# The second layer's MLP: in each quarter the first pair of down chunks takes eight of its 16 k tiles in seven products

## The chip, the cores and the metric

The kernel runs on one NeuronCore of a Trainium2 chip. The metric is the device time of one execution in microseconds (us), as the median of several runs. A profiled execution of the kernel before was also recorded; its own time is given below beside the medians.

The engines are named as in the profile: PE is TensorE (matmuls; PEld are its weight loads), DVE is VectorE, ACT is ScalarE, POOL is GpSimd, SP is SyncE, which issues most of the transfers from HBM.

## The reference

The reference is a decoder trunk of two layers on 256 tokens of width 2048, all in float32. Each layer has a token mixer (layer 0 a gated MLP with spatial mixing, layer 1 a state-space layer), a cross-attention to a memory of 256 tokens, and an MLP, each behind an RMS norm and with a residual add; a final RMS norm ends it. The change lies in the MLP of layer 1:

```python
def squared_relu_mlp(h, w_up, w_down):
    return jnp.square(jax.nn.relu(h @ w_up)) @ w_down
...
    x = x + squared_relu_mlp(rms_norm(x, g_ff[i]), f_w_up[i], f_w_down[i])
```

`h` is 256 x 2048, `w_up` 2048 x 8192, `w_down` 8192 x 2048.

## The kernel before, in words

**Float32 out of three matmuls.** Every float32 operand is split into a high part, which is the value cast to float32r, and a low part, which is the rest. A product is then high x high + low x high + high x low, three matmuls where one would do. `split` (L103, L104) makes the two parts: ScalarE casts the high part (`whi`, `own`, `hh`), VectorE subtracts it from the source for the low part (`wlo`, `own`, `hl`). Weights come from HBM in tiles of 128 x 1024 float32 (512 KB): two k tiles of 128 rows by 512 columns. They arrive in raw buffers `wraw` (four) and are split into `whi` and `wlo` (three buffers each).

**The MLP** (`mlp`, L630 on) goes through the 8192 hidden features in four quarters `b` of 2048. A quarter first computes its up products: four chunks `n` of 512 features, two calls of `gemm_feat` (L163 to L191) each, whose result is evicted by a copy on ScalarE and an add on VectorE, squared behind the relu (L649) and split into `hh` and `hl`, the tokens' operand of the down product. Then come the quarter's down products: the 2048 hidden features are 16 k tiles, the 2048 output columns are four chunks of 512, and each chunk's result is added to the residual `x` by `gather` (L666).

**Seven products.** In layer 1 the down chunks are taken in pairs by `gemm_seven` (L705 on), except for the last two chunks of the last quarter. For a pair the operands of the first four k tiles form a 2 x 2 by 2 x 2 block product: two token halves `t` of 128, two halves `i` of the k tiles (two k tiles each), two output chunks `j`. It would take eight block products; by the scheme of Strassen in Winograd's form it takes seven, four of them with sums of token blocks. A block product is six matmuls of 128 x 128 by 128 x 512 (two k tiles, three matmuls each). The k tiles behind the first four are taken straight (`direct`, `whole`): one weight tile serves both token halves, twelve matmuls.

The sums on the tokens' side are made once per quarter by `token_sums` (L691 on) from the first up chunk, and split: `sums`. The sums of weight blocks are made by VectorE as they are needed, in `run` and in one of the raw tiles `ws` (four buffers): run = B01 - B00, then run = B11 - run, B01 = B11 - B01, run = B10 - run. A weight block that meets `sums` is split into tiles `own`, of which there are two (L656):

```python
own = lambda: mp.tile([P, KB * NB], F32R, name="own", bufs=2)
```

`parts` takes one for the high and one for the low part, so that one such pair exists at a time. The other blocks go through `whi` and `wlo`. The products are, in the written order: 1 (`summed` 0, into the PSUM bank of token half 0 and chunk 1), 2 (`block`, bank (1, 0)), 3 (`block`, bank (0, 0)), 4 and 5 (`summed` 1 and 2, bank (1, 0)), 6 (`block`, bank (1, 0)), 7 (`summed` 3, bank (0, 1)). Between products 3 and 7 stand four direct tiles. What a bank holds after products 1, 2, 4 and 5 is also needed by itself: `keep` (L763) has ScalarE copy it to a tile `kept` of 128 x 512 before the next product adds to the bank. The copy after product 5 is `u3`:

```python
u3 = keep((1, 0), 3)
whole(0, 0)
v.tensor_tensor(out=run, in0=raw[1, 0], in1=run, op=ALU.subtract)
block((1, 0), 1, 1, run)
```

`whole(0, 0)` first writes bank (0, 0) with six matmuls, then bank (1, 0) with six.

**What sets the order.** The kernel is written as a flow of operations on tiles. A scheduler at build time orders the instructions of each engine by priority and by its own costs, hands out the buffers of the pools, and puts in the semaphore waits. Each engine then works through its list in that order, and a transfer waits in SP's list until its buffer is free. So the order on an engine can differ from the written one, and a change in one place can move its neighbours.

Of the kernel before, what the change touches and what calls it, by code (L numbers as in the profile page):

```python
# [16 lines left out]
P = 128  # L17
# [21 lines left out]
class Trunk:  # L39
# [454 lines left out]
    def attention(self, x, layer, cur, nxt):  # L494
# [3 lines left out]
        with tc.tile_pool(name="at", bufs=2, reuse_waits="tile") as ap:  # L498
# [67 lines left out]
            def values(h0):  # L566
# [16 lines left out]
                self.gemm_seven(tiles, token(memT), self.mem_sums, wv, h0, 0,  # L583
# [40 lines left out]
            for j in range(0, NCH, 2):  # L624
                self.gemm_seven(tiles, token(oT), sums[0], wo, j, 0, gather)
                for n in (j, j + 1):
                    self.at(1 + n - j, lambda n=n: nxt.chunk(x, n))


    def mlp(self, x, layer, cur, nxt):  # L630
# [3 lines left out]
        with tc.tile_pool(name="ml", bufs=4, reuse_waits="tile") as mp:  # L634
# [3 lines left out]
            kept = lambda i: mp.tile([P, NB], F32, name="kept", bufs=4)  # L638
            self.fifth = None if nxt.closing else mp
            for b in range(DFF // D):  # L640
                hid = []
                for n in range(NCH):
# [10 lines left out]
                    if nxt.closing and n == 0:  # L653
                        sums = self.token_sums(ws(), lambda: mp.tile([P, 4, 2, P], F32R, name="sums", bufs=2), *rs)
# [14 lines left out]
                for n in range(NCH):  # L669
                    end = b == DFF // D - 1  # L670
                    if nxt.closing and not (end and n >= NCH - 2):
                        if n % 2 == 0:
                            self.gemm_seven((ws, run, kept), lambda kt, t: [f[:, kt % 4, t * P:(t + 1) * P]
                                                                            for f in hid[kt // 4]],
                                            sums, wd, n, b * KT, gather, own=own)
                            if end:
                                nxt.start()
# [27 lines left out]
    def gemm_seven(self, tiles, token, sums, w, n0, k0, gather, end=None, own=None):  # L705
# [23 lines left out]
        def into(key, kts, left, hi, lo, end=False):  # L729
# [10 lines left out]
        def block(key, t, i, src, end=False):  # L740
            into(key, range(KB), lambda kk: token(KB * i + kk, t), *parts(src), end)

        def summed(key, k, src, end=False):
            into(key, range(KB), lambda kk: [f[:, k, kk, :] for f in sums], *parts(src, own), end)

        todo = {j: list(range(2, KT // KB)) for j in range(2)}
# [23 lines left out]
        run = run()  # L770
        v.tensor_tensor(out=run, in0=raw[0, 1], in1=raw[0, 0], op=ALU.subtract)
        summed((0, 1), 0, run, True)
        block((1, 0), 0, 0, raw[0, 0], True)
        m5, m1 = keep((0, 1), 0), keep((1, 0), 1)
        block((0, 0), 0, 1, raw[1, 0])
        whole(1, 1)
        v.tensor_tensor(out=run, in0=raw[1, 1], in1=run, op=ALU.subtract)
        summed((1, 0), 1, run, True)
# [4 lines left out]
        summed((1, 0), 2, raw[0, 1], True)  # L783
# [4 lines left out]
        block((1, 0), 1, 1, run)  # L788
        whole(1, 1)
        summed((0, 1), 3, raw[1, 1])  # L790
# [752 lines left out]
```

## Time and profile before

| | us |
|---|---|
| median of 3 runs | 2791.5 (2790.08 to 2792.14) |
| profiled execution, its own time | 2789.63 |
| span of its trace, first to last instruction | 2787.9 |

Busy time in the profiled execution: PE 99% of the span, DVE 71%, ACT 50%, POOL 8%; the granted PE clock is 0.999 of full speed, and the transfers run at 213 GB/s in the mean. The MLP of layer 1 takes the last quarter of the span: the four quarters' first pairs begin at 2170.34, 2344.19, 2518.05 and 2691.92 us from the span's start.

How to read the rows: a group of instructions has its line, engine, operation, output tile <- input tiles and shape, then the busy time and the mean in ns of one, then the idle time of its engine before it and who ended that. In a timeline a row has the start, the duration, engine, line and operation; in square brackets stands the idle time before and its releaser. The windows give the busy time of each engine in a stretch, with the number of its instructions. Matmuls overlap in time, so that their busy times do not add up to the time they take.

### The profile page before, as it was taken

Reading aid. Unit: us, or ns where it says so; the run is one execution under the profiler, and the core shown is the slowest. Engines: PE = TensorE matmul, PEld = TensorE weight load, DVE = VectorE, ACT = ScalarE, POOL = GpSimd, SP = SyncE. Lnnn points to the kernel's source line nnn. Section 1 sums busy time; section 2 is a strip of 40 time slices with the busy share of each in tenths; the row PEclk is TensorE's granted clock in tenths of the full one; section 3 lists DMA queues with packets and bytes.
Section 4 is the critical chain, followed back from the end, with each engine's and each line's share of the span. In section 5 each row is a group of like instructions: output and inputs, shape, how many; then the busy total and the mean of one; then the engine's idle time right before and its main releaser. Section 6 shows DMA issues by size and latency. Waiting matters only on the chain. (4 is left out here: it accounts for less than half of the span.)

```text
span 2787.9 us, 39690 instructions
## 1 busy us (share of the span) xinstructions
PE 2767.1 (99%) x15020; PEld 2331.6 (84%) x15020; DVE 1984.8 (71%) x2740; ACT 1396.2 (50%) x1805; POOL 234.4 (8%) x435
## 2 busy tenths in 40 slices
PE   9999999999999999999999999999999999999998
PEld 7888888888888888888887888888888888888887
DVE  6865756778978778787567657557776767667665
ACT  6545544554534434444556445445554545445454
POOL 0100000001022222221213100000000000000000
PEclk9999999999999999999999999999999999999999
DMA  8766655557788888887879767564556566565655
GB/s 294 232 209 217 200 179 181 175 158 244 211 260 260 255 259 262 257 259 226 240 242 270 217 199 239 176 191 159 179 158 216 170 212 204 164 221 167 213 187 158
DMA packets 196223, 593.76 MB, mean 213 GB/s; under 512 B 45120, under 2 KB 47216, under 8 KB 195520
## 3 DMA queue, kind: packets, MB, share of 16 engines
q1 hardware_dynamic: 151728, 531.17, 60.7%
q0 software_dynamic: 43776, 59.01, 7.8%
q8 instruction: 117, 1.92, 0.3%
q10 hardware_dynamic: 528, 1.06, 0.1%
q14 instruction: 74, 0.61, 0.1%
HBM read 567.51 MB, written 23.46 MB: 212 GB/s over the span
## 5 line engine op out<-in xcount | busy, mean ns | idle before, releaser
L104 DVE TENSOR_TENSOR wlo<-wraw,whi 128x1024 fp32r<-128x1024 f32 (+1 forms) x893 | 1085.9, 1221 | 490.4 <-ACT whi L103 484.8
L103 ACT CAST whi<-wraw 128x1024 fp32r<-128x1024 f32 (+1 forms) x893 | 937.3, 1052 | 857.0 <-PE acc L731 204.5
L174 PE MATMUL acc<-act,whi 128*128 128x512 f32 x3072 | 742.4, 392 | 0.6 <-ACT whi L103 0.6
L174 PEld LDWEIGHTS acc<-act,whi 128*128 128x128 f32 x3072 | 562.7, 188 | 111.5 <-issue 2.6
L179 PEld LDWEIGHTS acc<-act,wlo 128*128 128x128 f32 x3072 | 394.9, 191 | 18.6 <-DVE wlo L104 2.9
L179 PE MATMUL acc<-act,wlo 128*128 128x256 f32 x3072 | 403.9, 283 | 1.9 <-DVE wlo L104 1.5
L159 PE MATMUL acc<-whi,act 128*128 128x512 f32 x1472 | 369.8, 393 | 6.2 <-ACT whi L103 5.4
L159 PEld LDWEIGHTS acc<-whi,act 128*128 128x128 f32 x1472 | 275.1, 189 | 64.0 <-ACT whi L103 5.4
L731 PE MATMUL acc<-whi,act 128*128 128x512 f32 x864 | 233.0, 392 | 0.0
L815 PE MATMUL acc<-whi,hl 128*128 128x512 f32 x544 | 213.3, 392 | 0.0
L814 PE MATMUL acc<-whi,hh 128*128 128x512 f32 x544 | 212.7, 391 | 0.0
L159 PE MATMUL acc<-wlo,act 128*128 128x512 f32 x736 | 197.9, 391 | 0.0
L731 PEld LDWEIGHTS acc<-whi,act 128*128 128x128 f32 x864 | 160.3, 188 | 36.5 <-ACT ends L763 1.9
L159 PEld LDWEIGHTS acc<-wlo,act 128*128 128x128 f32 x736 | 138.6, 188 | 28.9
L731 PE MATMUL acc<-whi,hh 128*128 128x512 f32 x378 | 148.4, 393 | 0.0
L731 PE MATMUL acc<-whi,hl 128*128 128x512 f32 x378 | 147.1, 389 | 0.0
L817 PE MATMUL acc<-wlo,hh 128*128 128x512 f32 x544 | 145.9, 390 | 0.0
L731 PE MATMUL acc<-wlo,act 128*128 128x512 f32 x432 | 133.1, 390 | 0.0
L815 PEld LDWEIGHTS acc<-whi,hl 128*128 128x128 f32 x544 | 102.1, 188 | 23.1 <-issue 2.2
L190 ACT COPY r<-acc 128x512 f32<-128x512 f32 x64 | 37.6, 587 | 166.7 <-PE acc L174 166.7
L817 PEld LDWEIGHTS acc<-wlo,hh 128*128 128x128 f32 x544 | 102.1, 188 | 21.5 <-issue 0.2
L814 PEld LDWEIGHTS acc<-whi,hh 128*128 128x128 f32 x544 | 102.1, 188 | 21.4 <-issue 0.4
(369 smaller groups left out, 2762.4 us busy)
## 6 DMA issues: line engine op xcount, KB each, us to landing
wraw<-in_f_w_up SPq DMA_DIRECT2D x256, 512.0 KB, 4.6
wraw<-in_f_w_down SPq DMA_DIRECT2D x228, 512.0 KB, 4.6
wraw<-in_x_w_q SPq DMA_DIRECT2D x64, 512.0 KB, 4.1
wraw<-in_x_w_k SPq DMA_DIRECT2D x64, 512.0 KB, 4.4
wraw<-in_b_w_out SPq DMA_DIRECT2D x64, 512.0 KB, 4.4
wraw<-in_a_w_in SPq DMA_DIRECT2D x63, 512.0 KB, 4.1
wraw<-in_x_w_v SPq DMA_DIRECT2D x48, 512.0 KB, 4.2
wraw<-in_x_w_o SPq DMA_DIRECT2D x48, 512.0 KB, 4.3
```

What stands on the lines that cost most here:

```text
L103: self.nc.scalar.copy(out=hi, in_=src)
L104: return self.nc.vector.tensor_tensor(out=lo, in0=src, in1=hi.bitcast(F32), op=ALU.subtract).ins
L159: nc.tensor.matmul(out[t], a[:, kt, sl], b[:, kk, :], start=st and a is ah, stop=en)
L174: nc.tensor.matmul(acc[:, f, :], hi[:, kk, sl], both[:, kt].rearrange("p a s -> p (a s)"), start=first and kk == 0, stop=last and kk == FK ...
L179: nc.tensor.matmul(acc[:, f, 0:S], lo[:, kk, sl], ah[:, kt, :], start=False, stop=last and kk == FK - 1, skip_group_check=True)
L190: nc.scalar.copy(out=dst, in_=acc[:, :, S:])
L731: mm = lambda s, m, e: nc.tensor.matmul(out, s, m, start=key not in begun, stop=e, skip_group_check=True)
L814: nc.tensor.matmul(acc[:, t, :], ah, hi[:, kk, :], start=kt == 0, stop=False)
L815: nc.tensor.matmul(acc[:, t, :], al, hi[:, kk, :], start=False, stop=False)
L817: nc.tensor.matmul(acc[:, t, :], hid[kt // 4][0][:, kt % 4, sl], lo[:, kk, :], start=False, stop=kt == KT - 1)
```

## The change

In each quarter, the first pair of down chunks (`n` = 0) now takes eight of its 16 k tiles in seven products: the four k tiles behind the first four are a second block. Each of the seven products has two halves, one of either block, which add into the same bank. The second block's four raw weight tiles are loaded ahead by `block_ahead` into one large tile `more` (from the pool of the activations, whose buffer the attention has left), and three of its four weight sums are made there during the up products; the fourth is made in place in the GEMM. A second set of token sums comes from the second up chunk (`sums` has four buffers instead of two). The direct tiles of a first pair fall from twelve to eight. The `kept` tiles now lie in `more` too. The quarter's second pair is taken as before, with one block. In the attention the calls hand over the same sums as a list, which changes nothing there; those lines are left out below.

The scheduler places the rest. Three places in the first quarter's first pair, by engine, with output tile <- input tiles.

TensorE, from the fifth product (the third `summed`) to the work after it; the moving weights stand first, then the stationary tokens. Before:

```order
L731 MATMUL acc<-own,sums 128x512 x6
L731 MATMUL acc<-whi,hh 128x512
L731 MATMUL acc<-whi,hl 128x512
L731 MATMUL acc<-whi,hh 128x512
L731 MATMUL acc<-whi,hl 128x512
L731 MATMUL acc<-wlo,hh 128x512 x2
```

Now:

```order
L750 MATMUL acc<-own,sums 128x512 x6
L750 MATMUL acc<-wlo,hh 128x512 x2
L750 MATMUL acc<-own,sums 128x512 x6
L750 MATMUL acc<-whi,hh 128x512
L750 MATMUL acc<-whi,hl 128x512
```

The product's second half follows two matmuls behind its first, and the six matmuls with `hh` and `hl` that stood behind the product have moved ahead of it.

VectorE at the same place, with buffer numbers, since rows would read alike. Before:

```order
L104 TENSOR_TENSOR own_19905<-ws_19811,own_19904 128x1024
L666 SCALAR_TENSOR_TENSOR x_5605<-kept_19883,r2_18966,x_5605 128x512
L104 TENSOR_TENSOR wlo_19937<-run_19817,whi_19936 128x1024
L104 TENSOR_TENSOR wlo_19949<-wraw_19946,whi_19948 128x1024
L104 TENSOR_TENSOR own_19965<-ws_19815,own_19964 128x1024
```

Now:

```order
L104 TENSOR_TENSOR own_19959<-ws_19828,own_19958 128x1024
L673 SCALAR_TENSOR_TENSOR x_5605<-more_19605,r2_18966,x_5605 128x512
L795 TENSOR_TENSOR run_20146<-ws_20140,ws_20138 128x1024
L104 TENSOR_TENSOR wlo_20011<-more_19605,whi_20010 128x1024
L104 TENSOR_TENSOR own_19969<-more_19605,own_19968 128x1024
L104 TENSOR_TENSOR own_20039<-ws_19832,own_20038 128x1024
```

own_19905 was the low part of the fifth product's weights; own_19959 and own_19969 are those of its two halves, and between them now stand the next pair's first subtraction (L795) and the split of a tile for product 6 (wlo_20011).

ScalarE at the head of the GEMM; L190 is the copy that evicts the up's last product. Before:

```order
L103 CAST whi_19829<-ws_19809 128x1024
L103 CAST whi_19843<-ws_19813 128x1024
L190 COPY r_19693<-acc_19694 128x512
L103 CAST whi_19855<-wraw_19853 128x1024
L103 CAST own_19872<-run_19817 128x1024
L103 CAST hh_19596<-r_19693 128x512
```

Now:

```order
L103 CAST whi_19866<-more_19605 128x1024
L190 COPY r_19707<-acc_19708 128x512
L103 CAST whi_19878<-ws_19830 128x1024
L103 CAST own_19846<-more_19605 128x1024
L103 CAST hh_19610<-r_19707 128x512
L103 CAST whi_19888<-more_19605 128x1024
```

The cast for product 3, whi_19843, stood ahead of that copy; now whi_19878 stands behind it, followed by own_19846, the second half of product 1, and later whi_19888, the second half of product 3.

The diff:

```diff
--- before.py
+++ after.py
@@ -635,7 +635,7 @@
             r2 = mp.tile([P, 32 if layer else 56], F32, name="r2", bufs=1)[:, 0:2]
             ws = lambda: mp.tile([P, KB * NB], F32, name="ws", bufs=4)
             run = lambda: mp.tile([P, KB * NB], F32, name="run", bufs=1)
-            kept = lambda i: mp.tile([P, NB], F32, name="kept", bufs=4)
+            kept = lambda i: more[:, 6 + i // 2, i % 2 * NB:i % 2 * NB + NB]
             self.fifth = None if nxt.closing else mp
             for b in range(DFF // D):
                 hid = []
@@ -651,7 +651,14 @@
                         rs.append(r)
                     hid.append((h, l))
                     if nxt.closing and n == 0:
-                        sums = self.token_sums(ws(), lambda: mp.tile([P, 4, 2, P], F32R, name="sums", bufs=2), *rs)
+                        sums = []
+                    if nxt.closing and n < 2:
+                        sums.append(self.token_sums(ws(), lambda: mp.tile([P, 4, 2, P], F32R, name="sums", bufs=4), *rs))
+                    if nxt.closing and n == NCH - 2:
+                        more = self.act.tile([P, 8, KB * NB], F32, name="more", tag="act")
+                        ahead = self.block_ahead(more, wd, b * KT)
+                if nxt.closing:
+                    ahead[-1]()
                 if nxt.closing:
                     own = lambda: mp.tile([P, KB * NB], F32R, name="own", bufs=2)
                     nxt.room = lambda: mp.tile([P, 2, NB], F32, name="g", tag="ws", bufs=4)
@@ -672,7 +679,7 @@
                         if n % 2 == 0:
                             self.gemm_seven((ws, run, kept), lambda kt, t: [f[:, kt % 4, t * P:(t + 1) * P]
                                                                             for f in hid[kt // 4]],
-                                            sums, wd, n, b * KT, gather, own=own)
+                                            sums, wd, n, b * KT, gather, own=own, ahead=ahead if n == 0 else None)
                             if end:
                                 nxt.start()
                     elif nxt.closing and end and n == NCH - 1:
@@ -702,7 +709,19 @@
         self.split(sh, sl, s)
         return sh, sl
 
-    def gemm_seven(self, tiles, token, sums, w, n0, k0, gather, end=None, own=None):
+    def block_ahead(self, tile, w, k0):
+        v = self.nc.vector
+        raw = {(i, j): tile[:, 2 * i + j] for i in range(2) for j in range(2)}
+        for (i, j), t in raw.items():
+            self.fed = self.nc.sync.dma_start(out=t.rearrange("p (k c) -> p k c", k=KB), in_=w[j, k0 // KB + 2 + i]).ins
+
+        def add():
+            v.tensor_tensor(out=tile[:, 4], in0=raw[0, 1], in1=raw[0, 0], op=ALU.subtract)
+            v.tensor_tensor(out=tile[:, 5], in0=raw[1, 1], in1=tile[:, 4], op=ALU.subtract)
+            v.tensor_tensor(out=raw[0, 1], in0=raw[1, 1], in1=raw[0, 1], op=ALU.subtract)
+        return raw, tile[:, 4], tile[:, 5], add
+
+    def gemm_seven(self, tiles, token, sums, w, n0, k0, gather, end=None, own=None, ahead=None):
 
 
 
@@ -726,7 +745,7 @@
 
         begun = set()
 
-        def into(key, kts, left, hi, lo, end=False):
+        def into(key, kts, left, hi, lo):
             out = banks[key]
             mm = lambda s, m, e: nc.tensor.matmul(out, s, m, start=key not in begun, stop=e, skip_group_check=True)
             for kk in kts:
@@ -737,13 +756,17 @@
             for kk in kts:
                 mm(left(kk)[0], lo[:, kk, :], True)
 
-        def block(key, t, i, src, end=False):
-            into(key, range(KB), lambda kk: token(KB * i + kk, t), *parts(src), end)
-
-        def summed(key, k, src, end=False):
-            into(key, range(KB), lambda kk: [f[:, k, kk, :] for f in sums], *parts(src, own), end)
-
-        todo = {j: list(range(2, KT // KB)) for j in range(2)}
+        def block(key, t, i, src, more=None):
+            into(key, range(KB), lambda kk: token(KB * i + kk, t), *parts(src))
+            if ahead:
+                into(key, range(KB), lambda kk: token(KB * (2 + i) + kk, t), *parts(more))
+
+        def summed(key, k, src, more=None):
+            into(key, range(KB), lambda kk: [f[:, k, kk, :] for f in sums[0]], *parts(src, own))
+            if ahead:
+                into(key, range(KB), lambda kk: [f[:, k, kk, :] for f in sums[1]], *parts(more, own))
+
+        todo = {j: list(range(4 if ahead else 2, KT // KB)) for j in range(2)}
 
         def direct(j, first):
 
@@ -768,26 +791,29 @@
         for i, j in ((0, 0), (0, 1), (1, 0), (1, 1)):
             fetch(i, j)
         run = run()
+        far, t1, t2 = ahead[:3] if ahead else ({}, None, None)
         v.tensor_tensor(out=run, in0=raw[0, 1], in1=raw[0, 0], op=ALU.subtract)
-        summed((0, 1), 0, run, True)
-        block((1, 0), 0, 0, raw[0, 0], True)
+        summed((0, 1), 0, run, t1)
+        block((1, 0), 0, 0, raw[0, 0], far.get((0, 0)))
         m5, m1 = keep((0, 1), 0), keep((1, 0), 1)
-        block((0, 0), 0, 1, raw[1, 0])
+        block((0, 0), 0, 1, raw[1, 0], far.get((1, 0)))
         whole(1, 1)
         v.tensor_tensor(out=run, in0=raw[1, 1], in1=run, op=ALU.subtract)
-        summed((1, 0), 1, run, True)
+        summed((1, 0), 1, run, t2)
         gather(0, n0, m1)
         u2 = keep((1, 0), 2)
         whole(1, 1)
         v.tensor_tensor(out=raw[0, 1], in0=raw[1, 1], in1=raw[0, 1], op=ALU.subtract)
-        summed((1, 0), 2, raw[0, 1], True)
+        summed((1, 0), 2, raw[0, 1], far.get((0, 1)))
         gather(0, n0 + 1, u2)
         u3 = keep((1, 0), 3)
         whole(0, 0)
         v.tensor_tensor(out=run, in0=raw[1, 0], in1=run, op=ALU.subtract)
-        block((1, 0), 1, 1, run)
+        if ahead:
+            v.tensor_tensor(out=t1, in0=far[1, 0], in1=t2, op=ALU.subtract)
+        block((1, 0), 1, 1, run, t1)
         whole(1, 1)
-        summed((0, 1), 3, raw[1, 1])
+        summed((0, 1), 3, raw[1, 1], far.get((1, 1)))
         v.tensor_tensor(out=u3, in0=u3, in1=m5, op=ALU.add)
         whole(0, 0)
         gather(1, n0 + 1, u3)
```

More of the change, by code (lines that the diff above doesn't have):

```diff
@@ L581, in end @@
                                                    op0=ALU.mult, op1=ALU.subtract)
-                self.gemm_seven(tiles, token(memT), self.mem_sums, wv, h0, 0,
+                self.gemm_seven(tiles, token(memT), [self.mem_sums], wv, h0, 0,
                                 lambda t, n, part: more.update({(t, n): part}), end)
@@ L624, in attention @@
             for j in range(0, NCH, 2):
-                self.gemm_seven(tiles, token(oT), sums[0], wo, j, 0, gather)
+                self.gemm_seven(tiles, token(oT), sums, wo, j, 0, gather)
                 for n in (j, j + 1):
```

## The prediction

> **What bounds the kernel now.** I read the page first, then the second layer's MLP in windows, then single stretches of the timeline by engine.
>
> ```profile
> span 2787.9 us, 39690 instructions
> PE 2767.1 (99%) x15020; PEld 2331.6 (84%) x15020; DVE 1984.8 (71%) x2740; ACT 1396.2 (50%) x1805; POOL 234.4 (8%) x435
> ...
> L731 PE MATMUL acc<-whi,hh 128*128 128x512 f32 x378 | 148.4, 393 | 0.0
> ...
> core 0: us, PE busy (x) PEld busy (x) DVE busy (x) ACT busy (x) POOL busy (x), PEclk, DMA share, GB/s
> 2078.00:2170.00 92.00, 91.67 (x532) 80.88 (x531) 66.59 (x89) 48.27 (x65) 0.00 (x0) 1.00 0.64 207
> 2170.34:2212.76 42.42, 42.42 (x187) 34.76 (x186) 32.20 (x32) 22.80 (x26) 0.00 (x0) 1.00 0.59 187
> 2344.19:2386.61 42.42, 42.42 (x188) 34.76 (x186) 32.28 (x32) 22.81 (x26) 0.00 (x0) 1.00 0.59 186
> 2518.05:2560.48 42.43, 42.43 (x187) 34.76 (x186) 32.38 (x32) 22.80 (x26) 0.00 (x0) 1.00 0.57 186
> ```
>
> TensorE is busy throughout at the full granted clock (1.00). Each of the lower three windows starts with a quarter's first product and ends with the first product of its next pair: it holds the seven-product GEMM that changes, 186 matmuls (and the overlap of a neighbour). 42.42 / 186 is 0.228 us per matmul, not the 0.39 that the group row gives as mean. The timeline agrees: starts are 0.227 apart, each row lasts 0.39, so 0.16 of a matmul lies under the next.
>
> ```profile
> 2168.50 2.00 PE L174 MATMUL acc<-act,whi 128*128 128x512 f32 x8
> 2170.34 1.52 PE L731 MATMUL acc<-own,sums 128*128 128x512 f32 x6
> 2171.70 0.39 PE L731 MATMUL acc<-whi,hh 128*128 128x512 f32 x1
> 2171.93 0.39 PE L731 MATMUL acc<-whi,hl 128*128 128x512 f32 x1
> ...
> 2179.41 0.61 PE L731 MATMUL acc<-wlo,hh 128*128 128x512 f32 x2
> 2179.88 0.50 PE L731 MATMUL acc<-whi,hh 128*128 128x512 f32 x1
> 2180.22 0.39 PE L731 MATMUL acc<-whi,hl 128*128 128x512 f32 x1
> ...
> 2184.09 0.47 PE L731 MATMUL acc<-whi,hh 128*128 128x512 f32 x1
> 2184.40 0.39 PE L731 MATMUL acc<-whi,hl 128*128 128x512 f32 x1
> ```
>
> ScalarE and VectorE prepare every weight tile, and evict, in the order written for them:
>
> ```profile
> 2170.54 0.59 ACT L190 COPY r<-acc 128x512 f32<-128x512 f32 x1 [2.70 <-PE acc L174]
> 2171.02 1.05 ACT L103 CAST whi<-wraw 128x1024 fp32r<-128x1024 f32 x1
> 2171.97 1.05 ACT L103 CAST own<-run 128x1024 fp32r<-128x1024 f32 x1
> 2172.93 0.61 ACT L103 CAST hh<-r 128x512 fp32r<-128x512 f32 x1
> ...
> 2179.25 0.57 ACT L763 COPY kept<-acc 128x512 f32<-128x512 f32 x1
> ...
> 2171.16 0.69 DVE L191 TENSOR_TENSOR r<-acc,r 128x512 f32<-128x512 f32 x1 [2.06 <-ACT r L190]
> 2171.89 0.69 DVE L649 SCALAR_TENSOR_TENSOR r<-r 128x512 f32<-128x512 f32 x1
> 2172.50 1.22 DVE L104 TENSOR_TENSOR wlo<-wraw,whi 128x1024 fp32r<-128x1024 f32 x1
> 2173.63 0.68 DVE L104 TENSOR_TENSOR hl<-r,hh 128x512 fp32r<-128x512 f32 x1
> ...
> L763 ACT COPY kept<-acc x28: 570/577/595, 2173.4 to 2705.0; 128x512 f32<-128x512 f32 x28
> ...
> PEld acc L731: 3.4, 14
> ```
>
> From these rows I take: a 128x1024 cast 1.05, the next starting 0.95 after it began; a split's subtraction 1.22 (1.13 to the next); a copy out of PSUM 0.58; handing over 0.04 (the up's last matmul ends at 2170.50, the copy starts at 2170.54). A matmul that waited resumes 0.17 after its release: the copy of 2179.25 ends at 2179.82, the next matmul stands at 2180.22, one pitch after 2179.99. These are the only waits of TensorE left in the windows, two in each: 2179.88 to 2180.22 is 0.11 over a pitch, 2184.09 to 2184.40 is 0.08, some 0.2 together. The last row counts 14 of them, for copies into `kept`, in seven such GEMMs.
>
> **The change part by part.** Each quarter's first pair loses six matmuls: the second block of four k tiles, like the first, takes seven products of six matmuls where it took eight. Four quarters: 24 matmuls, 24 x 0.227 = **-5.4 us**. [...]
>
> Added work: in the up stretch three 128x1024 subtractions (1.22 each, the size of a split's), one more set of token sums (four additions of a quarter of that size, at most 4.9 together, and a split of 1.22). That is at most 9.8 us of VectorE against 25 us free in the 92 us row above; no gap expected, and whole it would cost 39 us. Inside the GEMM: seven splits where four were and one subtraction, 4 x 1.22 = 4.9 more on VectorE, 32.2 + 4.9 = 37.1 of some 41; ScalarE gets three casts more, 22.8 + 3.2. On the average both fit. But the order decides, since two halves now follow each other in one product, and a summed half needs tile `own`, which has two buffers, one high and one low part: the second half's cast cannot start until the first half's matmuls are through.
>
> TensorE, as the rows of the change show: in product 5 two matmuls stand between the two summed halves, and the six that went to another bank while ScalarE copied the product out (`u3`) have moved ahead, so the next matmul adds into the bank being copied. VectorE: own_19959 and own_19969 are the low parts of the two halves; between them stand the next pair's first subtraction (L795; it needs that pair's transfers) and wlo_20011, a split for product 6. ScalarE: product 3's cast stood ahead of the up's last eviction (COPY r); it is now whi_19878, behind it, and whi_19888 is its second half; own_19846 is product 1's second half. `whi` has three buffers, so whi_19878 waits for the up's last matmul, and product 3 is now the second work of the GEMM, six matmuls after the start, where it was the third, after twelve.
>
> Transfers. Each quarter's four block loads replace four loads of the same bytes, but stand on SP's queue ahead of others:
>
> ```profile
> wraw<-in_f_w_down SPq DMA_DIRECT2D x100, 512.0 KB, 4.1
> ws<-in_f_w_down SPq DMA_DIRECT2D x28, 512.0 KB, 6.1
> ...
> SPq L127 <- DVE wlo L104: 519.3, 208, 9.6
> SPq L719 <- DVE run L787: 2.4, 3, 0.8
> ```
>
> SP waits mostly for VectorE to free a raw buffer, so it is not the limit. In the first quarter the first block load waits for the attention's last reader of its buffer, with up loads queued behind it, and VectorE's first block subtraction waits for the load with the split of the last token features behind: +0.3, bounds 0 (landed in time) and 2 (the difference of the two medians). L795 needs a `ws` load that is issued when L811 ends: two PSUM copies, an update, a split and itself after product 2, 1.9 after product 4's first matmul by the rows above. I take 5.1 to its landing, midway.
>
> Walk through one quarter; T is 0 at its first matmul, or at the one named.
> - A, product 3. The up's last matmul ends at 0.16; copy 0.20 to 0.78, cast 0.70 to 1.75, resumed 1.92. TensorE is there at 6 x 0.227 = 1.36. Lost **0.56**.
> - B, product 1's second half: cast 1.65 to 2.70, resumed 2.87 against 1.92 + 0.91. Lost 0.04.
> - C, product 3's second half needs the buffer that VectorE still reads: L191 0.81 to 1.50, L649 to 2.22, split 2.15 to 3.37. Cast 3.42 to 4.47, resumed 4.64 against 4.24. Lost **0.40**.
> - D, product 4's second half (four matmuls of a direct tile lie between): 0.05 at its high part, 0.12 at its low. Product 7 is built alike. Twice **0.17**.
> - E, product 5's second half; T is 0 at the first half's last high matmul. It ends 0.39, cast 0.43 to 1.48, resumed 1.65; TensorE is there after five pitches, 1.13. Lost **0.52**. The low part: from product 4's start 31 matmuls and D's 0.17 make 7.2, so L811 ended at 1.9 - 7.2 = -5.3 and L795 starts at -0.2; it and the next split keep VectorE until 2.1 (two pitches of 1.13), split 2.1 to 3.32, resumed 3.49 against 1.65 + 0.91 = 2.56. Lost **0.93**; 0.34 were VectorE free.
> - F, the bank. Two matmuls later, 3.95, TensorE wants it. The last low matmul ends at 4.11; product 7's cast, released at 3.3, keeps ScalarE until 4.4; copy 4.33 to 4.92, resumed 5.09. Lost **1.14**, and 0.96 with ScalarE free.
>
> Sum 0.56 + 0.04 + 0.40 + 0.34 + 0.52 + 0.93 + 1.14 = 3.93 a quarter. The fourth has no next seven-product pair, so nothing of L795 stands in E: 0.6 less. 4 x 3.93 - 0.6 = **+15.1**. The present small waits go, 4 x 0.2 = **-0.8**. The first up stretch: **+0.3**.
>
> Net -5.4 + 15.1 - 0.8 + 0.3 = +9.2. The profiled execution took 2789.63 (span 2787.9), so 2798.8; the median of the runs is 1.9 above it: **2800.7 us**.
>
> **The rivals.**
> 1. Transfers decide at E: at 6.1 to landing L795 starts 1.0 later and the low part loses 1.9, in three quarters +2.9; with the first up stretch at its bound, +1.7 more: 2803.6 to 2805.3. For it: the 6.1 row. Against: the 4.1 row of the same size. Chance 0.17.
> 2. Only the gaps that no order of ScalarE and VectorE can spare remain, E's cast 0.52 and F's 0.96: 4 x 1.48 = 5.9, net -0.3, 2791.2: no change. For it: handing over is fast in every row. Against: the queues above are fixed, and A to D would all have to vanish. Chance 0.10.
> 3. TensorE stays the bound and everything is hidden, as it is nearly now: -5.4 - 0.8 = -6.2, **2785.3**, not slower. It decides if each cast is ready when TensorE arrives, that is, if copy, cast and split took at most the 0.45 to 1.36 that lie between; the rows say 0.58, 1.05, 1.22. [...] Chance 0.07. That the matmuls do not go away is excluded: TensorE's program has 24 fewer.
>
> **How the numbers follow.** The forecast has 0.66. Its own bounds: with VectorE and ScalarE free at E and F and nothing at B to D, 0.56 + 0.86 + 0.96 = 2.38 a quarter, +9.5 - 6.2 = 2794.8; upwards rival 1. The range 2793.5 to 2807 takes in rival 1 and leaves out rivals 2 and 3, 0.17. About 0.2% (5.6 us) is what a measurement of this kernel can tell from no change: slower 0.83, within 0.11 (rival 2 and a little of 3), faster 0.06.
>
> **What would show it.** The four windows from a quarter's first product to its next pair: 42.4 now, 42.4 - 0.2 - 1.4 + 3.9 = 44.7 by the walk; under 41 if all is hidden. TensorE's waits there should name ScalarE's casts of `whi` and `own`, VectorE's split of `own`, and ScalarE's copy into `more`, about a microsecond each time at F. I am wrong if the up stretches grow by more than 2 us in all, if the largest wait is not at E or F, or if the windows shrink.

## The result, and the profile after

The changed kernel takes **2798.5 us** (median of 7 runs, 2797.05 to 2803.57) against 2790.2 of the kernel before (7 runs, 2788.06 to 2792.14): the ratio is 1.0032, with a 95% interval from 1.0022 to 1.0042. It is slower, by 8.4 us; forecast were 9.2. The profiled execution took 2801.42, its span is 2799.7.

The windows of the changed kernel, from a quarter's first product to the first product of its next pair for quarters 1 to 3, and the rest of quarter 1:

```profile
core 0: us, PE busy (x) PEld busy (x) DVE busy (x) ACT busy (x) POOL busy (x), PEclk, DMA share, GB/s
2171.58:2218.70 47.12, 44.33 (x182) 34.06 (x180) 37.11 (x36) 26.04 (x29) 0.00 (x0) 0.96 0.38 124
2350.13:2394.53 44.40, 42.79 (x181) 32.94 (x180) 37.10 (x36) 26.05 (x29) 0.00 (x0) 1.00 0.41 130
2525.97:2570.33 44.36, 42.74 (x181) 32.93 (x180) 37.13 (x36) 26.07 (x29) 0.00 (x0) 1.00 0.41 131
2218.70:2350.13 131.43, 131.43 (x699) 113.48 (x698) 94.13 (x100) 63.78 (x71) 0.00 (x0) 1.00 0.66 212
```

The six matmuls are gone (180 instead of 186), and yet the windows are longer than 42.42. VectorE has 37.1 us of work and ScalarE 26.05, as forecast, so neither is full. The rest of a quarter lasts 131.43, to the hundredth what it was (2212.76 to 2344.19). The first quarter's window is longer than the others, and its granted clock is 0.96.

The spans differ by 11.8 us: 4.70, 1.98 and 1.93 in these windows, 1.93 in the last quarter (2701.76 to the end, 97.94 instead of 96.01), and 1.24 ahead of the first product. Of those 1.24, 0.54 lie in the first up stretch; the other 0.70 were there at its first matmul (2079.57 instead of 2078.87), in a part of the program that the change does not touch.

TensorE's waits in the second layer's MLP, by what ended them (sum, times, longest):

```profile
PE acc L750 <- ACT more L786: 3.5, 4, 0.9
PE acc L750 <- ACT whi L103: 1.8, 8, 0.3
PE acc L750 <- DVE own L104: 1.2, 1, 1.2
PE acc L750 <- ACT own L103: 0.9, 4, 0.2
```

These are the four kinds that the walk named, and ScalarE's copy into `more`, once in each quarter, has the largest sum. TensorE's timeline of the second quarter, first at the head of the GEMM, then at the fifth product:

```profile
2350.13 1.52 PE L750 MATMUL acc<-own,sums 128*128 128x512 f32 x6
2351.92 0.50 PE L750 MATMUL acc<-whi,hh 128*128 128x512 f32 x1 [0.26 <-ACT whi L103]
2352.25 0.39 PE L750 MATMUL acc<-whi,hl 128*128 128x512 f32 x1
...
2368.68 1.55 PE L750 MATMUL acc<-own,sums 128*128 128x512 f32 x6
2370.07 0.61 PE L750 MATMUL acc<-wlo,hh 128*128 128x512 f32 x2
2370.91 2.00 PE L750 MATMUL acc<-own,sums 128*128 128x512 f32 x6 [0.23 <-ACT own L103]
2373.80 0.50 PE L750 MATMUL acc<-whi,hh 128*128 128x512 f32 x1 [0.89 <-ACT more L786]
2374.13 0.40 PE L750 MATMUL acc<-whi,hl 128*128 128x512 f32 x1
```

How a loss is read: six pitches after 2350.13 is 2351.49, the next matmul stands at 2351.92, and the one behind it 0.33 later instead of 0.227: 0.43 + 0.11, some 0.53. The bracket counts only idle time after the end of a pipelined row, and so shows half of it. At F the last of the six starts at 2370.91 + 2.00 - 0.39 = 2372.52, the next at 2373.80: 1.05 over a pitch, and 0.11 behind it. ScalarE at F: the copy comes behind product 7's cast, as the walk had it.

```profile
2372.21 1.05 ACT L103 CAST own<-ws 128x1024 fp32r<-128x1024 f32 x1 [1.35 <-PE acc L750]
2373.16 0.58 ACT L786 COPY more<-acc 128x512 f32<-128x512 f32 x1
```

In the first quarter two things are added. VectorE, at the fifth product:

```profile
2191.19 1.23 DVE L795 TENSOR_TENSOR run<-ws 128x1024 f32<-128x1024 f32 x1 [1.18 <-DMA ws<-in_f_w_down]
2192.33 1.22 DVE L104 TENSOR_TENSOR wlo<-more,whi 128x1024 fp32r<-128x1024 f32 x1
2193.47 1.22 DVE L104 TENSOR_TENSOR own<-more,own 128x1024 fp32r<-128x1024 f32 x1
```

The next pair's first subtraction waits for its transfer, with the split of the fifth product's second half two places behind. Then, right after F, the matmuls run at half speed for one stretch (starts 0.43 apart instead of 0.227):

```profile
2198.22 0.63 PE L750 MATMUL acc<-whi,hh 128*128 128x512 f32 x1
2198.64 0.63 PE L750 MATMUL acc<-whi,hl 128*128 128x512 f32 x1
2199.07 0.63 PE L750 MATMUL acc<-whi,hh 128*128 128x512 f32 x1
```

### The profile page after: what moved, and what is told of

It is laid out like the page before. It is cut to its first block, busy times and chain, and to the rows that moved or that the text cites. A ratio compares the mean times of both kernels' runs of the same rounds, so it can differ in the third digit from the quotient of the medians.

```text
span 2799.7 us, 39717 instructions
## 1 busy us (share of the span) xinstructions
PE 2771.4 (99%) x14996; PEld 2326.1 (83%) x14996; DVE 2026.1 (72%) x2788; ACT 1413.3 (50%) x1821; POOL 235.3 (8%) x435
## 5 line engine op out<-in xcount | busy, mean ns | idle before, releaser
L104 DVE TENSOR_TENSOR wlo<-wraw,whi 128x1024 fp32r<-128x1024 f32 (+1 forms) x877 | 1066.0, 1221 | 439.9 <-ACT whi L103 433.9
L103 ACT CAST whi<-wraw 128x1024 fp32r<-128x1024 f32 (+1 forms) x877 | 920.7, 1051 | 825.2 <-PE acc L750 182.4
L841 PE MATMUL acc<-whi,hl 128*128 128x512 f32 x544 | 213.3, 392 | 0.0
L840 PE MATMUL acc<-whi,hh 128*128 128x512 f32 x544 | 212.7, 391 | 0.0
L750 PE MATMUL acc<-whi,hh 128*128 128x512 f32 x338 | 134.0, 396 | 5.3 <-ACT more L786 3.5
L750 PE MATMUL acc<-whi,hl 128*128 128x512 f32 x338 | 132.2, 391 | 0.0
L190 ACT COPY r<-acc 128x512 f32<-128x512 f32 x64 | 37.7, 588 | 167.0 <-PE acc L174 167.0
```

The costliest lines, as they stand in the source:

```text
L103: self.nc.scalar.copy(out=hi, in_=src)
L104: return self.nc.vector.tensor_tensor(out=lo, in0=src, in1=hi.bitcast(F32), op=ALU.subtract).ins
L190: nc.scalar.copy(out=dst, in_=acc[:, :, S:])
L750: mm = lambda s, m, e: nc.tensor.matmul(out, s, m, start=key not in begun, stop=e, skip_group_check=True)
L840: nc.tensor.matmul(acc[:, t, :], ah, hi[:, kk, :], start=kt == 0, stop=False)
L841: nc.tensor.matmul(acc[:, t, :], al, hi[:, kk, :], start=False, stop=False)
```

## The experiments

Every kernel was timed in several rounds beside the kernel before. "Period" is the time from a quarter's first product to the next quarter's, read from the starts of TensorE's matmuls in each trace; "up 1" is the time from the first up stretch's first matmul to the first product. (Where the expectations speak of a quarter of 172.1 to 174.3, they count 0.46 less, two pitches, than these periods.) The ratio compares all the runs of both kernels, not their two medians.

| kernel | median, us | ratio to before (95%) | up 1 | periods 1, 2, 3 |
|---|---|---|---|---|
| before | 2790.2 (beside kernels 1 to 4), 2790.0 (5 to 8), 2790.8 (9, 10) | | 91.47 | 173.85, 173.86, 173.87 |
| the change | 2798.5 | 1.0032 (1.0022 to 1.0042) | 92.01 | 178.55, 175.83, 175.80 |
| 1 all second halves in `whi` | 2787.4 | 0.9989 (0.9981 to 0.9998) | 92.31 | 172.54, 172.57, 172.55 |
| 2 product 1 alone | 2797.6 | 1.0025 (1.0017 to 1.0034) | 91.75 | 175.23, 175.61, 174.85 |
| 3 products 1, 4, 7 | 2795.3 | 1.0017 (1.0008 to 1.0026) | 92.91 | 174.19, 174.57, 176.74 |
| 4 loads and sums alone | 2791.5 | 1.0003 (0.9994 to 1.0011) | 92.11 | 173.86, 173.88, 173.83 |
| 5 products 4 and 5 | 2789.7 | 1.0003 (0.9994 to 1.0012) | 92.71 | 173.72, 173.73, 173.69 |
| 6 change, copy thrice | 2808.7 | 1.0069 (1.0057 to 1.0082) | 91.46 | 179.15, 177.20, 177.17 |
| 7 as 1, copy thrice | 2793.4 | 1.0013 (1.0004 to 1.0022) | 92.23 | 173.89, 173.97, 173.90 |
| 8 as 1, sums on GpSimd | 2786.4 | 0.9987 (0.9978 to 0.9995) | 93.39 | 172.55, 172.53, 172.54 |
| 9 as 1, sums later | 2785.4 | 0.9980 (0.9971 to 0.9989) | 91.45 | 172.53, 172.54, 172.53 |
| 10 as 3, subtraction later | 2790.0 | 0.9994 (0.9985 to 1.0002) | 91.93 | 173.63, 173.63, 173.63 |

The medians carry a spread of some 2 us from the untouched part of the program (its first up matmul stands anywhere from 2078 to 2082 in these traces), so the small differences are read from the periods.

**1. All second halves through `whi` and `wlo`.** Two more `own` tiles would be the direct test; no run has them. Here the second halves go where three buffers exist.

```diff
-                into(key, range(KB), lambda kk: [f[:, k, kk, :] for f in sums[1]], *parts(more, own))
+                into(key, range(KB), lambda kk: [f[:, k, kk, :] for f in sums[1]], *parts(more))
```

> In every summed product the second half's weights are split into whi and wlo (three buffers each) instead of own (one pair); nothing else is edited. Theory (the time is lost in waits that come from the one own pair and from the order that follows from it): product 1's second half is ready early, product 2 comes before product 3, the halves of products 4, 5 and 7 no longer wait for each other. What is left is -5.4 for the matmuls, -0.8 for the old waits, +0.5 for the first up stretch and at most 0.2 a quarter of waits for copies, as before: 5 to 5.7 below the kernel before, 2784.5 to 2785.2, ratio 0.998. Rival 'added work' (seven splits, eight subtractions and four loads a quarter cost what they cost, whatever the buffers): within 2 us of the changed kernel, 2796.5 to 2800. Rival 'only the halves' (own explains B, D, E and G, but A, C and the bank copy F stand by themselves): the waits of 0.17 + 0.50 + 0.34 + 0.17 a quarter and the 1.2 in the first quarter go, 5.9 in all: 2792.6.

TensorE's table of waits is empty for the second layer's MLP, and the period is 172.54, 1.31 below before: 6 x 0.227 = 1.36 for the matmuls. VectorE, ScalarE and the transfers have the same work as in the changed kernel, so the rival "added work" falls, and so does "only the halves". The median is 2 us above what was expected. The first up stretch, 92.31, is 0.84 longer than before where 0.5 was expected. In the profiled execution another 1.40 lie ahead of that stretch (its first matmul at 2080.28 instead of 2078.87), in the untouched part.

**2, 3 and 5. Parts of it.** The same line, with the other buffers for some products only (`k` is 0 for product 1, 1 and 2 for products 4 and 5, 3 for product 7): `k in (0,)` in kernel 2, `(0,1,3)` in kernel 3, `(1,2)` in kernel 5.

```diff
-                into(key, range(KB), lambda kk: [f[:, k, kk, :] for f in sums[1]], *parts(more, own))
+                into(key, range(KB), lambda kk: [f[:, k, kk, :] for f in sums[1]], *parts(more, None if k in (0,) else own))
```

> As the run before, but only in product 1; products 4, 5 and 7 keep own for both halves. Theory: the waits at the head of the GEMM (0.53 and 0.45 a quarter in the trace of the changed kernel) come from product 1's second half, which could not be prepared and so drew product 3 forward: they go, 4 x 0.98 = 3.9, and those of products 4, 5, 7 and the bank copy stay: 2798.5 - 3.9 = 2794.6, ratio to the kernel before 1.0016. Rival 'only the halves': product 1's halves lost nothing in the trace, so nothing changes: 2798.5. Rival 'added work': 2798.5.

> The second halves of products 1, 4 and 7 through whi and wlo; product 5 alone keeps own for both halves. Theory: what is left is at product 5: the split of its second half (0.34 to 0.6 a quarter) and the bank copy F (1.16 a quarter): 0.5 + 4 x 1.5 to 1.8 - 5.4 - 0.8 = 0.3 to 1.5 above the kernel before, ratio 1.0001 to 1.0005, 2790.5 to 2791.7; the trace has one cluster of waits of TensorE in each quarter, ended by ScalarE's copy into more, about 1.1 us. Rival 'only the halves': D, G and nothing else go, 8 x 0.17 = 1.4: 2797.1.

> The complement of the second run: the second halves of products 4 and 5 through whi and wlo, those of products 1 and 7 through own. Nothing at the bank copy is edited. Theory (the waits belong to places, each with its own cause in own's one pair and the order that follows): the head of the GEMM stays as in the changed kernel (0.53 + 0.45 a quarter) and product 7's 0.17; D 0.17, E 0.50 + 0.34 and F 1.16 go, 8.7 in all, and the late load of the first quarter with them, 1.2: 2798.5 - 8.7 to 9.9 = 2788.6 to 2789.8, ratio 0.9994 to 0.9998; a quarter lasts 172.1 + 1.0 to 1.2 from first product to first product. Rival 'the bank copy stands by itself': F's 1.16 a quarter stays, 4.6: 2793.3 or more, a quarter 174.3.

TensorE's waits in kernel 2:

```profile
PE acc L750 <- ACT more L786: 3.5, 4, 0.9
PE acc L750 <- DVE own L104: 1.2, 2, 0.8
PE acc L750 <- ACT own L103: 0.9, 4, 0.2
```

Against the changed kernel the row for casts of `whi`, 8 times, is gone: A and C, both. Neither belongs to product 1, but with its second half ready early, product 2 stands ahead of product 3 again, and product 3's casts have time. The third period is 0.95 below the changed kernel's, 0.98 were expected; the second is only 0.22 below. The median fell by 0.9, not 3.9: the row for `DVE own` shows late splits in two quarters (the subtraction L795 waited for transfers there, 1.2 in all). So the time does not tell this kernel from the change; the trace does.

In kernel 3:

```profile
PE acc L750 <- ACT more L786: 3.3, 4, 0.9
PE acc L750 <- DVE own L104: 1.8, 3, 1.1
```

One cluster a quarter, as expected, but at 4 us more than expected: the late split costs 0.43, 0.80 and 1.36 in quarters 1 to 3, and 0.10 in the fourth, and the third period holds a stretch of half clock (starts 0.43 apart from 2544.82 to 2546.53). Kernel 10 takes this up.

In kernel 5:

```profile
PE acc L750 <- ACT whi L103: 1.8, 8, 0.3
```

The complement: A and C stay, and E and F are gone, though nothing was done to the copy or its bank. Behind product 5 stand six matmuls again, which by the written order go into bank (0, 0), and the copy (2369.78 to 2370.36) runs beside them:

```profile
2368.63 0.61 PE L750 MATMUL acc<-wlo,sums 128*128 128x512 f32 x2
2369.08 0.39 PE L750 MATMUL acc<-whi,hh 128*128 128x512 f32 x1
...
2369.99 0.61 PE L750 MATMUL acc<-wlo,hh 128*128 128x512 f32 x2
2370.44 0.47 PE L750 MATMUL acc<-whi,hh 128*128 128x512 f32 x1
```

So F is not a price of the copy: the second half of product 5 was so late that the work which had covered the copy was set ahead of it. The periods of kernels 2 and 5 add up: -0.95 and -2.10 of the changed kernel's 175.8, and product 7's 0.17, make 172.6; kernel 1 has 172.55.

**4. Loads and sums alone.** No GEMM uses the second block; the transfers, sums and token sums in the up stretches are made as in the change.

```diff
-                                            sums, wd, n, b * KT, gather, own=own, ahead=ahead if n == 0 else None)
+                                            sums, wd, n, b * KT, gather, own=own, ahead=None)
```

> The second block is loaded, its three sums and the token sums of the second up chunk are made and split during the up products, but no GEMM uses them: all pairs run as in the kernel before, with one block, and 24 matmuls come back. It prices the added work outside the GEMM. Theory: only the first up stretch grows, +0.3 to +0.6: 2790.5 to 2790.8, ratio 1.0001 to 1.0002. Rival 'added work': of the 13.8 us by which the changed kernel is above a change that hides everything, a good part stands here, 4 us or more: over 2794.

The periods are those of the kernel before, and the first up stretch is 0.64 longer. The added work outside the GEMM costs that and nothing more.

**6 and 7. The copy lengthened.** The copy `u3` is made three times, once in the changed kernel and once in kernel 1.

```diff
+        keep((1, 0), 3)
+        keep((1, 0), 3)
         u3 = keep((1, 0), 3)
```

> The changed kernel, with ScalarE's copy u3 of product 5's bank made three times instead of once: the wait F is lengthened by two copies of 0.58 (0.49 to 0.58 each), everything else as in the changed kernel. 'Waits add up' (a stall costs its own length): 4 x 1.0 to 1.2 = 4.0 to 4.6 more, 2802.5 to 2803.1, no stretch of half clock beyond the ones of the changed kernel. 'Clustered waits also cost clock' (in the traces so far a grid of 3.41 us stretches, and where TensorE sat idle for about 0.58 of one or more, the next ran at half clock): the waits E and F now hold some 3 us within 4.5, so the stretch behind them runs at half clock in most quarters, 1.6 more each: 2806 to 2809.5, and the profile shows three or four stretches of 3.4 us at 0.5 in the second layer's MLP.

> The same two extra copies in the kernel of the first run (all second halves through whi and wlo), where the wait at the copy stands alone. Both theories: a wait of 1.2 to 1.4 at the copy in each quarter, 4 x 1.1 to 1.3 = 4.5 to 5.2 above the first run's 2787.4, 2791.9 to 2792.6, and no half clock in the second layer's MLP, since 1.4 is 0.41 of a stretch. If a half clock comes there all the same, the rule read from the traces is wrong.

ScalarE and TensorE in kernel 6, first quarter:

```profile
2195.38 1.81 ACT L786 COPY more<-acc 128x512 f32<-128x512 f32 x3
...
2197.24 0.53 PE L750 MATMUL acc<-whi,hh 128*128 128x512 f32 x1 [2.11 <-ACT more L786]
```

Three copies take 1.81, one took 0.58, and F grows by as much: 1.23. Second and third period grow by 1.37 each, so a wait here costs its own length and little else. That makes 5 of the 10 us between kernel 6 and the changed kernel. For the rest no cause is shown. It has the size of about three more stretches of half clock, and the median lies in the range expected for them (2806 to 2809.5); but the profile shows two in the MLP, in the first quarter (clock 0.50 from 2197.60 to 2201.02) and in the fourth (which lasts 100.6 against 97.94; 1.4 of that is the longer wait), where three or four were expected, and the first quarter of the changed kernel's profile has one too. The granted clock of the timed runs is 0.9974 in the mean, against 0.9987 for the changed kernel. One stretch of half clock lowers it by 0.0006 (half of 3.41 in some 2800), so these clocks speak for one or two stretches more; that is an estimate, since they are given to 0.001. Kernel 7, where the same wait (1.0 in its row, 1.31 with the pitch) stands alone, has none, as expected (its periods are 1.35 to 1.40 above kernel 1's); its median is 0.8 above the range that was expected:

```profile
PE acc L750 <- ACT more L786: 4.2, 4, 1.0
```

**8 and 9. The first up stretch.** Both start from kernel 1. Kernel 8 makes the three subtractions on GpSimd; kernel 9 keeps them on VectorE and ties the first to the third up chunk.

```diff
+        v = self.nc.gpsimd
+
         def add():
             v.tensor_tensor(out=tile[:, 4], in0=raw[0, 1], in1=raw[0, 0], op=ALU.subtract)
```

```diff
                         ahead = self.block_ahead(more, wd, b * KT)
+                        c = rs[0][:, 0, 0:1]
+                        nc.vector.tensor_tensor(out=more[:, 4, 0:1], in0=c, in1=c, op=ALU.add)
```

> The kernel of the first run, with the three subtractions of the second block in the up stretch made by GpSimd instead of VectorE. Theory (VectorE's queue stands behind the subtraction that waits for its load, and in the first quarter the splits of the up weights with it, so the first up stretch grew by 0.2 to 1.4 in the five traces, 0.84 in the first run): the first up stretch is back at 91.5 from 92.3, nothing else changes: 0.5 to 0.9 below the first run's 2787.4, 2786.5 to 2786.9. Rival 'the load itself' (the up loads queued behind the block loads are late, whoever subtracts): no change, 2787.4. Rival 'GpSimd in the way' (its subtraction slows VectorE's own, or ends too late for product 1): the up stretches grow by over 1 us each, 2791 or more.

> The kernel of the first run, with a one-column addition (0.1 to 0.2) on VectorE that writes into the place of the second block's first sum from the third up chunk's result: so the block subtractions can no longer stand ahead of that chunk, long after their loads have landed; engine, loads and everything else as there. Theory (VectorE's queue stood behind a subtraction that waited for its load, and held the token features or splits that TensorE needs): the first up stretch, 92.3 there, is back at the 91.5 of the kernel before, and the four quarters stay at 172.1: 0.8 below the first run, 2786.6. Rival 'the up loads are late behind the block loads': still 92 or more, 2787.4.

GpSimd and VectorE in kernel 8 (its L721 is L719 of the change):

```profile
2089.37 2.38 POOL L721 TENSOR_TENSOR more<-more 128x1024 f32<-128x1024 f32 x1 [368.42 <-DMA more<-in_f_w_down]
...
2089.37 3.46 DVE L104 TENSOR_TENSOR wlo<-wraw,whi 128x1024 fp32r<-128x1024 f32 x1
```

The split beside GpSimd's subtraction takes 3.46 instead of 1.22, and TensorE waits 1.6 for the token features behind it: the first up stretch is 1.1 longer than in kernel 1, not shorter. The later quarters do not feel it (172.5). The median, 2786.4, lay just below the expected 2786.5 to 2786.9 all the same; that was luck, since the stretch went the other way.

With the subtractions 50 us later, in kernel 9, the stretch is 91.45, that of the kernel before, though the loads stand in the same queue. That alone does not settle the cause, because kernel 6, with the subtraction in its old place, has 91.46 too. The first subtraction's wait for its load does (kernel 1, then kernel 6):

```profile
2091.72 1.23 DVE L719 TENSOR_TENSOR more<-more 128x1024 f32<-128x1024 f32 x1 [1.27 <-DMA more<-in_f_w_down]
2091.14 1.22 DVE L719 TENSOR_TENSOR more<-more 128x1024 f32<-128x1024 f32 x1 [0.42 <-DMA more<-in_f_w_down]
```

In the change and in kernels 1, 2, 3 and 6 VectorE waits 0.96, 1.27, 0.71, 1.87 and 0.42 there, and the stretch is longer than before by that wait less 0.42 or 0.43. So in these five the subtraction at the head of VectorE's queue passed a late landing on to TensorE; the loads by themselves cost nothing in kernel 9.

Kernel 9's windows:

```profile
core 0: us, PE busy (x) PEld busy (x) DVE busy (x) ACT busy (x) POOL busy (x), PEclk, DMA share, GB/s
2170.18:2211.28 41.10, 41.10 (x181) 33.56 (x180) 35.62 (x35) 25.86 (x29) 0.00 (x0) 1.00 0.47 154
2342.71:2383.81 41.10, 41.10 (x182) 33.55 (x181) 35.63 (x35) 25.86 (x29) 0.00 (x0) 1.00 0.49 153
2515.25:2556.35 41.10, 41.10 (x182) 33.56 (x181) 35.62 (x35) 25.86 (x29) 0.00 (x0) 1.00 0.48 153
```

180 matmuls at 0.228: all but some 0.23 of small waits is hidden. Its median, 2785.4, is the lowest of the kernels, and the ratio 0.9980 (0.9971 to 0.9989) puts it below the kernel before as well as the changed one.

**10. The next pair's subtraction later.** In kernel 3, `run` gets a column that depends on the sum made of `u3`, so that L795 cannot stand ahead of the fifth product's second split.

```diff
+                                            late=more[:, 7, NB:NB + 1] if n else None)
...
+        if late is not None:
+            v.tensor_tensor(out=run[:, 0:1], in0=late, in1=late, op=ALU.add)
```

> The kernel of the third run (product 5 alone keeps own for both halves), with a one-column addition into run that reads the sum of u3: so the next pair's first subtraction, L795 of the changed kernel, comes behind product 5 on VectorE and not ahead of its second split. Theory (the low part of product 5's second half waits for VectorE, which waits for the next pair's transfer): TensorE's wait for DVE own, 0.43, 0.80 and 1.36 in the first three quarters of the third run, falls to 0.10 as in its fourth, where no such subtraction exists, and F falls to the 0.94 of that quarter; a quarter then lasts 173.1 to 173.3 without a half clock: 2.9 less, and 1.6 more less where a half clock went, 2790.8 to 2792.4. Rival 'the split is late because its cast is late': nothing changes, 2795.3.

VectorE of kernel 3 in its third quarter, then TensorE's waits of kernel 10 (its lines are one or two further down):

```profile
2537.82 1.23 DVE L795 TENSOR_TENSOR run<-ws 128x1024 f32<-128x1024 f32 x1 [1.31 <-DMA ws<-in_f_w_down]
...
2540.10 1.22 DVE L104 TENSOR_TENSOR own<-more,own 128x1024 fp32r<-128x1024 f32 x1
```

```profile
PE acc L751 <- ACT more L787: 2.7, 4, 0.7
```

The waits for `DVE own` are gone in all three quarters, F is 0.94, and each period is 173.63. The median fell by 5.2, of which 2.9 are waits, by their lengths; 1.6 is one stretch of half clock that kernel 3's profile had, and how often the timed runs had it is not known. The late split was a matter of VectorE's queue behind a transfer, as the walk had it.

## Why the prediction was right, point by point

(The expectations call product 7's loss G.)

| loss of TensorE, us | forecast | quarter 1 | quarters 2, 3 | quarter 4 |
|---|---|---|---|---|
| A, product 3's cast | 0.56 | 0.53 | 0.53 | 0.53 |
| B, product 1's second half | 0.04 | 0 | 0 | 0 |
| C, product 3's second half | 0.40 | 0.46 | 0.45 | 0.45 |
| D and product 7's | 0.34 | 0.33 | 0.33 | 0.33 |
| E, cast | 0.52 | 0.51 | 0.51 | 0.51 |
| E, low part | 0.93 (0.33 in the fourth) | 1.51 | 0.34 | 0.35 |
| F, the bank | 1.14 | 1.16 | 1.16 | 1.16 |
| half clock | none | 1.6 | 0 | 0 |

The losses are read as at A and F above, from the starts of the matmuls.

- **The matmuls** (-5.4) came as forecast: kernel 9, where 0.23 of small waits stand in each window as 0.2 did before, shows them by themselves, -1.32 a quarter. **The small waits** (-0.8) are gone from the changed kernel, but that gain was made up again by something in no term: between the losses its matmuls start 0.2281 apart in the mean instead of 0.2269, some 0.19 a quarter.
- **A, C, D, F and E's cast** agree to 0.06. They rest on durations of single rows and on the fixed order of the queues. Kernels 2 and 5 confirm the cause, and go beyond the prediction: A, C and F, which the walk gave causes of their own (a queue, a third buffer, a bank), all go when the second half of a summed product is free of `own`. One shortage had set the order of its neighbours. No run has more `own` tiles, so that these alone would do is not shown.
- **E's low part** is the term that was mis-sized. The step was: "I take 5.1 to its landing, midway." In the trace of the change the transfer, issued 13.75 after the first product, had landed 4.6 after its issue in the second and third quarter, and then L795 cost nothing (0.34 remained, which was my sum with VectorE free); in the first quarter the last of its 16 parts came after 5.7, and 1.51 were lost. So the landing is not one number: it changes from quarter to quarter, and kernels 2, 3 and 10 show that this term goes with it. Rival 1 (transfers decide at E) held in one quarter of three.
- **The first up stretch**: forecast 0.3, bounds 0 and 2. Measured 0.54 in the change, and from 0 to 1.44 in the other traces with the first subtraction at that place; VectorE's wait there and kernel 9 confirm the mechanism.
- **The half clock** was in no term. It cost 1.6 in the profiled first quarter: eight matmuls, from 2197.39 to 2200.78, took 3.39 where eight pitches are 1.82. Without it and without the 0.70 of the untouched part the profiled difference of 11.8 is 9.5, against 9.2. So close an agreement is in part luck: the losses of the table come to 14.5 instead of 15.1, and the longer pitch (0.8 in all) and the first up stretch (0.2 over its term) make up for it.
- **The median** was put 1.9 above the profiled execution, as in the first three runs; over seven runs the median of before is 2790.2, 0.6 above it. That is most of the 2.2 us between forecast and result.
- Rivals 2 and 3 need A to D hidden; they were not. Rival 3's figure, 2785.3, is nearly kernel 9's 2785.4, by chance in part: in the same rounds the kernel before took 2790.8, so that 5.4 were gained and not 6.2.

## What to carry to other kernels

On a path that is busy 99% of the time, count which operand is ready when, product by product: engines with 15% to 40% of free time cost 3.3 to 4.5 us a quarter here through order and through one pair of buffers. When two halves are put side by side into a product, give the second half other buffers than the first; here the rest of the order then repaired itself. And see what an engine's queue holds behind an instruction that waits for a transfer: a subtraction that could have been made 50 us later was worth 0.9 us in the first up stretch (92.31 to 91.45).

## What was not expected of the hardware

**Stretches of half clock.** Between the start and the end of the kernel, TensorE's clock records in the changed kernel show two stretches of 3.41 us at half clock, which begin 686.1 us apart, 201 times 3.413. In the stretch of that length ahead of each, TensorE was busy for about half of the time (windows, changed kernel):

```profile
core 0: us, PE busy (x) PEld busy (x) DVE busy (x) ACT busy (x) POOL busy (x), PEclk, DMA share, GB/s
1507.90:1511.32 3.42, 1.67 (x11) 0.99 (x9) 3.28 (x10) 3.09 (x9) 1.20 (x3) 1.00 0.61 187
1511.32:1514.73 3.41, 3.19 (x8) 2.51 (x9) 3.38 (x7) 1.25 (x3) 2.85 (x5) 0.50 0.81 253
2193.99:2197.40 3.41, 1.78 (x7) 1.17 (x8) 2.24 (x3) 1.53 (x2) 0.00 (x0) 1.00 0.00 0
2197.40:2200.81 3.41, 3.41 (x10) 2.63 (x9) 2.25 (x3) 1.69 (x2) 0.00 (x0) 0.50 0.52 159
```

The first is in the token mixer, which the change does not touch. The kernel before has the same waits there, but stretches counted in steps of 3.413 from its first clock record fall otherwise on them:

```profile
1509.44:1512.85 3.41, 1.86 (x7) 1.26 (x8) 3.27 (x9) 3.01 (x7) 0.65 (x2) 1.00 1.01 262
1512.85:1516.26 3.41, 3.41 (x17) 2.82 (x16) 3.38 (x8) 1.06 (x1) 1.78 (x4) 1.00 0.95 256
```

Kernel 6 in its first and its second quarter:

```profile
2194.19:2197.60 3.41, 1.09 (x4) 0.61 (x5) 1.75 (x3) 2.70 (x4) 0.00 (x0) 1.00 0.00 0
2197.60:2201.02 3.42, 3.42 (x10) 2.64 (x9) 1.92 (x3) 1.04 (x1) 0.00 (x0) 0.50 0.54 158
2371.67:2375.08 3.41, 1.94 (x7) 0.97 (x6) 2.23 (x3) 2.03 (x4) 0.00 (x0) 1.00 0.04 14
2375.08:2378.50 3.42, 2.47 (x11) 2.03 (x12) 2.04 (x4) 1.92 (x3) 0.00 (x0) 1.00 0.51 149
```

In these windows half clock followed 1.09, 1.67 and 1.78 us of TensorE, and did not follow 1.86 and 1.94. (The expectation of kernel 6 took a stretch idle for 0.58 of its length; 1.78 busy is one idle for 0.48.) In the token mixer the kernel before has some 3.41 us with only 1.42 of TensorE and the changed kernel some with 1.44, if the stretch is laid where it is least; the half clock came in the changed kernel alone. At 1.6 us a stretch, as in the first quarter, that could part two executions of one kernel by as much; this is an estimate, and no run here was made to show it, nor what sets the clock.

**VectorE beside GpSimd.** A split of 1.22 took 3.46 beside a subtraction of the same size on GpSimd (kernel 8, rows above). Beside GpSimd's second subtraction an addition of L191 took its usual 0.69, and the operation of L649 behind it 1.42 instead of 0.69; the cause is not shown.

```profile
2093.85 2.41 POOL L722 TENSOR_TENSOR more<-more 128x1024 f32<-128x1024 f32 x1 [2.10 <-DMA more<-in_f_w_down]
...
2094.66 0.69 DVE L191 TENSOR_TENSOR r<-acc,r 128x512 f32<-128x512 f32 x1 [0.97 <-ACT r L190]
2095.39 1.42 DVE L649 SCALAR_TENSOR_TENSOR r<-r 128x512 f32<-128x512 f32 x1
```
